# A list scheduler's cost table: the drain of an instruction booked as latency, and a short look ahead on each engine

## The chip, the cores and the metric

The kernel runs on one core of a Trainium2 chip. The metric is the device time of one launch in microseconds (us), the median of several runs. Engines are named as in the profile: PE is the matrix engine (PEld its weight loads), DVE the vector engine, ACT the scalar engine, POOL the GpSimd engine, SP the sync engine, which issues nearly all DMAs here.

## The reference

One layer of a hybrid decoder serves 256 prompt tokens and 8 sequences of 8 new tokens, 320 tokens in all, with D_MODEL 2048. One wide projection feeds two recurrent branches, each branch is projected back, and the two are merged by gates:

```python
h = rms_norm(x, norm_g)
p = jnp.einsum('nld,dp->nlp', h, w_in)          # 2048 -> 11392 columns
...
y_a, s_a_new = rwkv7_recurrence(r_h, heads_a(decay), k_h, v_h, kk, heads_a(a), s_a)
...
o_b, s_b_new = gla_chunkwise(heads_b(q_b, DK_B), heads_b(k_b, DK_B), heads_b(i_b, DV_B),
                             heads_b(log_g, DK_B), s_b)
...
merged = (jax.nn.sigmoid(p[..., OFF_GA:OFF_GB].astype(f32))
          * jnp.einsum('nlw,wd->nld', y_a.astype(dt), proj_a)
          + jax.nn.sigmoid(p[..., OFF_GB:].astype(f32))
          * jnp.einsum('nlw,wd->nld', y_b.astype(dt), proj_b))
y = x + jnp.einsum('nld,de->nle', merged.astype(dt), w_out)
```

## The kernel before

All big products are made with three passes of a reduced float type: a weight tile `raw` (1024 rows by 128 columns, 512 KB) is loaded by SP, ACT casts it to its high part `whi`, DVE subtracts to get the low part `wlo`, and PE multiplies high by high, high by low and low by high. One such half tile is a block of 24 matmuls into a PSUM tile `mps`. These 320-column matmuls are called stream matmuls here.

The program has four stages. In the start stage the input is normalized and transposed and a first tile is made. In the recorded stage eight rounds run, p = 0 to 7. Each projects eight column tiles (r, k, v, za, q, f, i, zb: sixteen blocks) and then has the work of both branches for that round: `rwkv(p, ...)` for two heads of branch A and `hgrn(p, ...)` for one head of branch B. That work is a long chain of small steps: small matmuls and transposes on PE into the PSUM tiles `a`, `b` and `y`, with DVE, ACT and POOL steps between them. Seven gate tiles follow. In the third stage the remaining gates, proj_a (`ppa`), proj_b (`ppb`) and the merge are made, from lines 362 to 364 (matmuls), 352 (cast) and 353 (subtraction). The last stage is the output projection (`po`) and the final norm.

Only the recorded stage is ordered by a planner, class `Recorder`. It records every call of a round on every engine (all carry line 1465, where the recorded calls are issued again) and then orders them once, before the program is built:

- `add` gives each operation a cost (how long it holds its engine) and a latency `lat` (how much later a reader on its result may start).
- `link` builds the dependences. An edge marked as data adds the latency. `rank` is the longest way to the end.
- `order` is a list scheduler. `choose(e)` picks for engine e the next operation: for PE a ready small matmul, otherwise the next stream matmul; for the other engines, among the operations that could start within 30 ns of the earliest one, the one with the greatest `worth`. Worth puts the weight split of a block first when fewer than 4500 ns of stream matmuls are left ahead of it, then the operation with the greatest rank, and splits that are not urgent last.
- `OVER` says how early an operation may start on the SBUF port that DVE and POOL share, `MARGIN` is 250 ns added in front of a small matmul.

What the planner emits is a fixed order for each engine. The engines run through their own orders on the chip and wait for one another by semaphores, so a planned time that is wrong changes nothing by itself; it only puts an instruction in a worse place. PE has its stream matmuls to fill the time that a chain of branch work needs: the number of stream matmuls that stand between two dependent small matmuls is the cover of the steps between them.

Names that the text below uses: `uE<-a`, `uB<-a`, `pp`, `yz`, `yd` belong to a triangular solve of branch A that goes back and forth between PE and the other engines; `dn`, `pp<-scr`, `y`, `ye` are a small inverse in the same branch whose pieces are rearranged by two round trips through DRAM (`scr<-dn` then `pp<-scr`, and `scr<-y` then `ye<-scr`), after which POOL writes `yd` and PE transposes it (`a<-ident,yd`).

Of the kernel before, what the change touches and what calls it, by code (L numbers as in the profile page):

```python
# [67 lines left out]


class Recorder:  # L70
    APART, MARGIN, WAIT, OVER = 10, 250, 6000, 130
    LAT = {"PE": 215, "V": 45, "S": 45, "G": 80, "Y": 0}

    def __init__(self, engines, is_big):
        self.real, self.ops, self.spans, self.is_big = engines, [], {}, is_big
# [10 lines left out]
    def add(self, eng, name, fn, args, kw):  # L86
        o = Op()
        o.eng, o.fn, o.args, o.kw, o.n = eng, fn, args, kw, len(self.ops)
        aps = [x for x in (*args, *kw.values()) if hasattr(x, "start_partition")]
        out = aps[0]  # L90
        free = 1
        for d in out.shape[1:]:
            free *= d
        o.uses = []
        for j, x in enumerate(aps):
            t_ = x.tensor
            if "DRam" in type(t_).__name__:
                if t_.name.startswith("scr"):
                    o.uses.append((t_.name, 0, 1, 1, j == 0, False))
                continue  # L100
            key = (t_.name, x.offset, tuple(map(tuple, x.ap)))
            if key not in self.spans:
                self.spans[key] = span_of(x)
            o.uses.append((*self.spans[key], j == 0, "PSUM" in str(x.space)))
        o.lat = self.LAT[eng]
        o.dma = "dma" in name
        o.mode = None
        o.block, o.group = self.block, self.group
        o.margin, o.wait = 0, self.wait

        two = sum("PSUM" not in str(x.space) for x in aps[1:] if tuple(x.shape[1:]) != (1,)) > 1
        o.hold = two and eng in "VG"
        o.port = two and eng == "V" or eng == "G" and "dma" not in name
        if eng == "PE":
            lhs, rhs = aps[1], aps[2]
            o.cols = 1
            for d in lhs.shape[1:]:
                o.cols *= d
            n = 1
            for d in rhs.shape[1:]:  # L120
                n *= d
            up = lambda x: 32 if x <= 32 else 64 if x <= 64 else 128
            o.mode = up(lhs.shape[0]), 128 if name == "transpose" else up(o.cols)
            one = name == "transpose" or lhs.dtype == F32R
            o.passes = 1 if one else 2
            load = o.cols / 1.2
            stream = n / 2.4 + 13 if one and lhs.dtype == F32R else 2 * n / 2.4
            side = 128 // o.mode[1] * (128 // o.mode[0] if o.group else 1)
            o.cost = o.passes * max(max(load, stream) / side, 7) if o.group else o.passes * max(load, stream / min(2, side))
            if o.mode == (128, 128) and n > 256:  # L130
                o.cost = o.passes * stream
            o.stream = self.is_big(out)
            o.margin = 0 if o.stream else self.MARGIN
        elif eng == "V":
            two = name in ("tensor_scalar", "tensor_copy") and all(not u[5] for u in o.uses)
            o.cost = (free / 2 if two else free) / 0.96 + (150 if two else 157)
            if two:
                o.hold = o.port = True
            if any(tuple(x.shape[1:]) == (1,) and free > 1 for x in aps[1:]):
                o.cost += 55  # L140
            if name == "tensor_tensor_scan":
                o.cost = 2 * free / 0.96 + 157
        elif eng == "S":
            o.cost = (150 if name == "copy" else 200) + free / 1.2
            if name == "copy" and not o.uses[1][5]:
                o.cost += 40
            if any(tuple(x.shape[1:]) == (1,) and free > 1 for x in aps[1:]):
                o.cost += 60
        elif eng == "G":
            o.cost = 950 if "dma" in name else 95 + free * 0.88 if name == "memset" else 200 + free * 1.66  # L150
            if "dma" in name:
                o.lat = 4500
        else:
            o.cost, o.lat = 380, 2600 if any(u[0].startswith("scr") for u in o.uses) else 5500
        self.ops.append(o)
        return o

    def link(self):
# [42 lines left out]
        for o in self.ops:  # L201
            o.npred = len(preds[o.n])
            for q, data in preds[o.n].values():
                q.succ.append((o, data))
        for o in reversed(self.ops):
            o.rank = o.cost + max((q.rank + (o.lat if data else 0) for q, data in o.succ), default=0)
        for members in groups.values():
# [4 lines left out]
    def order(self):  # L212

        self.link()
        free = dict.fromkeys(self.real, 0.0)
# [7 lines left out]
        port = {"V": 0.0, "G": 0.0}  # L223
# [6 lines left out]
        def choose(e):  # L230

            q = ready[e]
            now = free[e]
            if e in port:
                held = port["G" if e == "V" else "V"] - self.OVER
                if e == "V" and held > now and port["G"] == free["G"]:

                    held += min((o.cost for o in ready["G"] if o.hold and o.ready <= free["G"] - 40), default=0.0)
                at_ = {o: max(now, o.ready, held if o.port else 0.0) for o in q}
                t_ = min(at_.values())  # L240
            else:
                t_ = max(now, min(o.ready for o in q))
            if e == "PE":
                can = [o for o in q if o.ready <= t_ + 1]
                own = [o for o in can if o.mode == mode and not o.stream]
                part = [o for o in can if o.mode != (128, 128)]
                if mode != (128, 128):
                    near = [o for o in q if o.mode == mode and o.ready <= t_ + 60]
                    pool = own or near or part or can
                elif own:  # L250
                    pool = own
                elif part and (run_ >= self.APART and any(t_ - o.ready >= o.wait for o in part) or len(part) == len(can)):
                    pool = part
                else:
                    pool = [o for o in can if o.stream]
                o = max(pool, key=lambda o: (o.rank, -o.n))
                if o.stream:
                    o = min((o for o in pool if o.stream), key=lambda o: o.n)
                return max(t_, o.ready), o
            can = [o for o in q if (at_[o] if e in port else o.ready) <= t_ + 30]  # L260

            def worth(o):
                if o.block is None:
                    return (3 if e == "Y" else 1), o.rank
                slack = (at[o.block] - gone) * 147 + max(0, free["PE"] - t_)
                return (2 if slack < 4500 else 0), -o.n
            return t_, max(can, key=worth)

        while left:
            t_, o = min((choose(e) for e in ready if ready[e]), key=lambda x: (x[0], x[1].eng == "V"))  # L270
# [1413 lines left out]
```

## Time and profile before

| | us |
|---|---|
| runs: median (lowest to highest of 3) | 1105.28 (1103.35 to 1106.14) |
| the profiled execution | 1104.54 |
| its span, first to last instruction | 1102.8 |
| PE busy | 1081.3 |
| DVE busy | 750.6 |
| ACT busy | 680.1 |
| POOL busy | 154.6 |

The profiled execution took 1.7 us more than its span, which lies outside its first and last instruction. Busy times are unions over an engine's instructions, so two that overlap are counted once. The recorded stage lies at about 27 to 690 us, the third stage follows to about 1000 us, the output projection after that. In a row of the timeline the first number is the start, the second the length, and a bracket at the end gives the idle time ahead of the row and what ended it.

### The profile page before, as it was taken

What the parts mean: (1) busy time and instruction counts of PE and PEld (TensorE: products, weight loads), DVE (VectorE), ACT (ScalarE), POOL (GpSimd) and SP (SyncE); (2) the same over time, 40 slices, a digit from 0 to 9 for tenths busy, and PEclk for the clock granted to TensorE, in tenths of its full rate; (3) what the DMA queues carried; (4) which work ended last, traced back from release to release, by engine and by line L of the source; (5) the groups of instructions that cost most, each with busy time, mean ns of one, the idle gap of its engine ahead of it and who ended that gap; (6) DMA issues with size and microseconds to landing.
All of it is one profiled execution on the core that took longest, in us unless ns stands there. A gap on an engine that the chain in (4) does not pass through costs nothing.

```text
span 1102.8 us, 23134 instructions
## 1 busy us (share of the span) xinstructions
PE 1081.3 (98%) x9020; PEld 1043.5 (95%) x9020; DVE 750.6 (68%) x1639; ACT 680.1 (62%) x1530; POOL 154.6 (14%) x328
## 2 busy tenths in 40 slices
PE   7999999999999999999999999999999999999996
PEld 6999999999998999999999999999999999998886
DVE  8878787888787788788887976644444444437532
ACT  8767776766865867857857867544444444435412
POOL 6421222311211211211311210000000000000000
PEclk9999999999999999999999999999999999999999
DMA  6743644654553554555445454555555555586502
GB/s 200 205 127 100 180 129 123 161 145 114 162 136 101 156 144 117 153 138 140 117 138 144 123 144 130 149 152 160 152 146 146 149 154 153 153 282 223 200 21 96
DMA packets 298386, 161.62 MB, mean 147 GB/s; under 512 B 37341, under 2 KB 288480, under 8 KB 297700
## 3 DMA queue, kind: packets, MB, share of 16 engines
q1 hardware_dynamic: 297908, 158.83, 50.1%
q8 instruction: 71, 1.16, 0.4%
q10 hardware_dynamic: 368, 1.31, 0.3%
q14 instruction: 39, 0.32, 0.1%
HBM read 149.41 MB, written 10.70 MB: 145 GB/s over the span
## 4 chain that ended last, share of the span: by engine, by line
PE 95%; ACT 2%; DMA 1%; DVE 1%; issue 0%; POOL 0%; DVEq 0%; SPq 0%; ACTq 0%
PE mps L1465 45%; PE a L1465 9%; PE mps L362 5%; PE mps L364 5%; PE mps L363 5%; PE b L1465 3%; PE po L1555 3%; PE po L1556 3%; PE po L1557 3%; PE ppa L363 2%; PE ppa L364 2%; PE ppa L362 2%; PE ppb L362 2%; PE ppb L363 2%; PE ppb L364 2%; PE y L1465 1%
## 5 line engine op out<-in xcount | busy, mean ns | idle before, releaser
L1465 PE MATMUL mps<-hhi,wlo 128*128 128x320 f32 x1136 | 358.9, 316 | 0.0
L1465 PE MATMUL mps<-hhi,whi 128*128 128x320 f32 x1136 | 357.0, 314 | 0.5 <-ACT pad L1465 0.5
L1465 PE MATMUL mps<-hlo,whi 128*128 128x320 f32 x1136 | 357.3, 314 | 0.0
L1465 PEld LDWEIGHTS mps<-hhi,wlo 128*128 128x128 f32 x1136 | 213.7, 188 | 2.3 <-issue 1.5
L1465 PEld LDWEIGHTS mps<-hhi,whi 128*128 128x128 f32 x1136 | 213.8, 188 | 2.0 <-issue 0.8
L1465 PEld LDWEIGHTS mps<-hlo,whi 128*128 128x128 f32 x1136 | 213.7, 188 | 1.5 <-issue 0.8
L1465 DVE TENSOR_TENSOR wlo<-raw,whi 128x1024 fp32r<-128x1024 f32 x140 | 173.6, 1240 | 21.0 <-ACT whi L1465 19.7
L1465 ACT CAST whi<-raw 128x1024 fp32r<-128x1024 f32 x140 | 146.4, 1045 | 63.2 <-PE mps L1465 56.7
L352 ACT CAST whi<-raw 128x1024 fp32r<-128x1024 f32 x82 | 86.0, 1049 | 147.8 <-PE mps L363 94.3
L353 DVE TENSOR_TENSOR wlo<-raw,whi 128x1024 fp32r<-128x1024 f32 x82 | 100.5, 1225 | 110.1 <-ACT whi L352 110.1
L362 PE MATMUL mps<-hhi,whi 128*128 128x320 f32 x400 | 123.9, 310 | 1.0 <-ACT whi L352 1.0
L364 PE MATMUL mps<-hhi,wlo 128*128 128x320 f32 x400 | 123.7, 309 | 0.2 <-DVE wlo L353 0.2
L363 PE MATMUL mps<-hlo,whi 128*128 128x320 f32 x400 | 123.8, 309 | 0.0
L362 PEld LDWEIGHTS mps<-hhi,whi 128*128 128x128 f32 x400 | 75.1, 188 | 1.3 <-ACT whi L352 1.3
L364 PEld LDWEIGHTS mps<-hhi,wlo 128*128 128x128 f32 x400 | 75.1, 188 | 0.4 <-DVE wlo L353 0.4
L363 PEld LDWEIGHTS mps<-hlo,whi 128*128 128x128 f32 x400 | 75.2, 188 | 0.0
L1544 DVE TENSOR_TENSOR wlo<-raw,whi 128x1024 fp32r<-128x1024 f32 x32 | 38.4, 1222 | 36.0 <-ACT whi L1543 35.8
L1543 ACT CAST whi<-raw 128x1024 fp32r<-128x1024 f32 x32 | 33.1, 1052 | 47.7 <-PE po L1560 21.1
L1555 PE MATMUL po<-whi,mhi 128*128 128x512 f32 x128 | 50.0, 391 | 0.0
L1556 PE MATMUL po<-whi,mlo 128*128 128x512 f32 x128 | 50.0, 391 | 0.0
L1557 PE MATMUL po<-wlo,mhi 128*128 128x512 f32 x128 | 50.0, 391 | 0.0
L362 PE MATMUL ppa<-yah,whi 128*128 128x320 f32 x128 | 40.1, 314 | 0.1
(444 smaller groups left out, 2100.2 us busy)
## 6 DMA issues: line engine op xcount, KB each, us to landing
raw<-in_w_in_dram SPq DMA_DIRECT2D x194, 512.0 KB
raw<-in_w_out_dram SPq DMA_DIRECT2D x32, 512.0 KB
raw<-in_proj_a_dram SPq DMA_DIRECT2D x16, 512.0 KB
raw<-in_proj_b_dram SPq DMA_DIRECT2D x16, 512.0 KB
s<-in_state_hgrn_dram SPq DMA_DIRECT2D x8, 512.0 KB
out_dram<-s SPq DMA_DIRECT2D x8, 512.0 KB
s<-in_state_rwkv_dram SPq DMA_DIRECT2D x8, 256.0 KB
out_dram<-s SPq DMA_DIRECT2D x8, 256.0 KB
```

The costliest lines, as they stand in the source:

```text
L352: S.copy(hi[:, ks], raw[:, ks])
L353: sub.tensor_sub(lo[:, ks], raw[:, ks], hi[:, ks].bitcast(F32))
L362: T.matmul(dst, hi[:, q, :], xhi[:, k, :], start=(k == 0), stop=False)
L363: T.matmul(dst, hi[:, q, :], xlo[:, k, :], start=False, stop=False)
L364: T.matmul(dst, lo[:, q, :], xhi[:, k, :], start=False, stop=(k == nk - 1))
L1465: o.fn(*o.args, **o.kw)
L1543: S.copy(hi, raw)
L1544: V.tensor_sub(lo, raw, hi.bitcast(F32))
L1555: T.matmul(pt, h, hi, start=first, stop=False)
L1556: T.matmul(pt, l, hi, start=False, stop=False)
L1557: T.matmul(pt, h, lo, start=False, stop=end)
```

## The change

In the table of `Recorder`, the cost of a DVE, ACT or POOL instruction is lowered by 85, 100 or 65 ns (`DRAIN`), and the same number is added to its latency. The latencies themselves are trimmed from 45, 45 and 80 ns to 40, 40 and 65. `OVER` goes from 130 to 45, which is the same point in time, since the end that it is counted from is 85 ns earlier. `tensor_reduce` is now charged for the elements that it reads, not only for those that it writes.

In `link`, an edge from a DVE, ACT or POOL operation to another engine always carries the latency, also where only a buffer is handed back.

In `choose`, an engine other than PE now looks 150 ns ahead (`AHEAD`, before 30). When the operation with the greatest worth is ready only later than 30 ns from now, one that is ready and will be done at most 60 ns (`SLIP`) after that point goes first; if there is none, the engine is kept free for it. No operation is added or removed.

```diff
-    APART, MARGIN, WAIT, OVER = 10, 250, 6000, 130
-    LAT = {"PE": 215, "V": 45, "S": 45, "G": 80, "Y": 0}
+    APART, MARGIN, WAIT, OVER = 10, 250, 6000, 45
+    AHEAD, SLIP = 150, 60
+    LAT = {"PE": 215, "V": 40, "S": 40, "G": 65, "Y": 0}
+    DRAIN = {"V": 85, "S": 100, "G": 65}
...
+        if eng in self.DRAIN and not o.dma:
+            if name == "tensor_reduce":
+                n = 1
+                for d in aps[1].shape[1:]:
+                    n *= d
+                o.cost += (n - free) / 0.96
+            o.cost -= self.DRAIN[eng]
+            o.lat += self.DRAIN[eng]
...
-                q.succ.append((o, data))
+                q.succ.append((o, data or q.eng in self.DRAIN and q.eng != o.eng))
...
-            can = [o for o in q if (at_[o] if e in port else o.ready) <= t_ + 30]
+            if e not in port:
+                at_ = {o: max(now, o.ready) for o in q}
...
-            return t_, max(can, key=worth)
+            best = max((o for o in q if at_[o] <= t_ + self.AHEAD), key=worth)
+            if at_[best] > t_ + 30:
+                short = [o for o in q if at_[o] <= t_ + 30 and at_[o] + o.cost <= at_[best] + self.SLIP]
+                if short:
+                    best = max(short, key=worth)
+            return t_, best
```

The recorded calls keep their number, and their lines move by 16 (1465 becomes 1481, 352 becomes 368). Three places show what the planner makes of it.

On PE, in round 7 of 8, the triangular solve alternates between `a<-pp,uB` and `a<-yz,uE`. Before, the rows there read:

```order
L1465 MATMUL a_496<-yz,uE_504 128x128 x2
L1465 MATMUL mps<-hhi,wlo 128x320
L1465 MATMUL a_497<-pp_515,uB_501 128x128 x2
L1465 MATMUL mps<-hhi,whi 128x320
L1465 MATMUL mps<-hlo,whi 128x320
L1465 MATMUL a_496<-yz,uE_504 128x128 x2
L1465 MATMUL a_498<-ident,yd 128x128 x2
```

The same two steps from `a<-pp,uB` to `a<-yz,uE` on PE in the changed program:

```order
L1481 MATMUL a_497<-pp_515,uB_501 128x128 x2
L1481 MATMUL mps<-hlo,whi 128x320
L1481 MATMUL mps<-hhi,wlo 128x320
L1481 MATMUL mps<-hhi,whi 128x320
L1481 MATMUL mps<-hlo,whi 128x320
L1481 MATMUL b_526<-ident,i_487 128x128 x3
L1481 MATMUL mps<-hhi,wlo 128x320
L1481 MATMUL mps<-hhi,whi 128x320
L1481 MATMUL a_496<-yz,uE_504 128x128 x2
L1481 MATMUL a_498<-ident,yd 128x128 x2
```

Between the two steps stood two stream matmuls; now there stand six and three transposes of branch B. Ahead of `a<-pp,uB` stood one stream matmul, now eleven. At the same step of round 6, where two stream matmuls stood between `a<-pp,uB` and `a<-yz,uE` a second time, now stand fourteen. The new order repeats itself: in rounds 2 to 7 these distances are the same each time, which they were not before.

On DVE, in round 3, the small inverse is nine steps from `y<-id,pp` to the second reduction. Before, from the first of them:

```order
L1465 TENSOR_TENSOR y_0_517<-id_146,pp_515 96x64
L1465 TENSOR_TENSOR F_529<-F_529 128x16x8
L1465 TENSOR_TENSOR pp_515<-y_0_517 96x4
L1465 TENSOR_TENSOR w_0_524<-w_0_524,f_485 128x320
L1465 TENSOR_TENSOR wlo<-raw,whi 128x1024
L1465 TENSOR_TENSOR y_0_517<-y_0_517,pp_515 96x2x2
L1465 TENSOR_TENSOR R_530<-R_530,F_529 128x8x16
L1465 TENSOR_TENSOR pp_515<-y_0_517 96x4
```

DVE in the changed program, round 3, the whole inverse and a row on either side:

```order
L1481 TENSOR_TENSOR wlo<-raw,whi 128x1024 x2
L1481 TENSOR_TENSOR y_0_517<-id_146,pp_515 96x64
L1481 TENSOR_TENSOR pp_515<-y_0_517 96x4
L1481 TENSOR_TENSOR y_0_517<-y_0_517,pp_515 96x2x2
L1481 TENSOR_TENSOR pp_515<-y_0_517 96x4
L1481 TENSOR_TENSOR y_0_517<-y_0_517,pp_515 96x2x2
L1481 TENSOR_TENSOR pp_515<-y_0_517 96x64
L1481 TENSOR_REDUCE p_0_518<-pp_515 96x16
L1481 TENSOR_TENSOR pp_515<-y_0_517,p_0_518 96x64
L1481 TENSOR_REDUCE y_0_517<-pp_515 96x4x4
L1481 TENSOR_TENSOR q_483<-q_483,w_0_524 128x320
```

Two weight splits (`wlo`) and eight other steps stood among the nine; now they stand ahead of them and behind them. The stretch of PE that this chain has to fit into, from the `a<-arp,bk` that it starts from to the first `a<-ident,yd`, held 130 stream matmuls in round 1 and 159 to 174 in rounds 2 to 8; now it holds 127 in rounds 1 to 7 and 120 in round 8. On SP a `raw` load stood between `scr<-y` and `ye<-scr` in six of the eight rounds and between `scr<-dn` and `pp<-scr` in three; now it does in eight and in seven.

On ACT, at the end of the recorded stage, the last steps of round 8 (the group norm, `uB`) stood among the first casts of the third stage (line 352):

```order
L1465 ACTIVATE f_485<-mps 128x320
L1465 COPY uE_504<-a_496 128x320
L1465 ACTIVATE f_485<-f_485 128x320
L1465 ACTIVATE uB_501<-a_496 128x320
L1465 ACTIVATE f_485<-f_485 128x320
L1465 CAST rh_494<-uB_501 128x320
L1465 COPY ks_537<-b_527 100x128
L352 CAST whi<-raw 128x1024
L1465 ACTIVATE uB_501<-a_497,eps_g 128x320
L1465 ACTIVATE uB_501<-uB_501 128x320
L352 CAST whi<-raw 128x1024
L1487 CAST yah<-ya 128x640 x4
```

ACT in the changed program, up to the same split of `ya` (line 1503 now):

```order
L1481 CAST whi<-raw 128x1024 x2
L1481 ACTIVATE za_481<-mps 128x320
L1481 ACTIVATE za_481<-za_481 128x320 x2
L1481 CAST whi<-raw 128x1024
L368 CAST whi<-raw 128x1024
L1481 ACTIVATE q_483<-mps 128x320
L1481 ACTIVATE q_483<-q_483 128x320 x2
L368 CAST whi<-raw 128x1024 x2
L1481 ACTIVATE f_485<-mps 128x320
L1481 ACTIVATE f_485<-f_485 128x320 x2
L368 CAST whi<-raw 128x1024
L1503 CAST yah<-ya 128x640 x4
```

The last branch work has left this place: on PE the last small matmul stood behind 76 stream matmuls of the third stage, and now stands 226 stream matmuls ahead of the end of the recorded ones. The number of times that PE changes between its full and its divided array is 64 in both programs.

## The prediction

> **What bounds the kernel now.** I read the page first, then the table of windows, then PE's own timeline at each place where a window shows it idle.
>
> ```profile
> PE 1081.3 (98%) x9020; PEld 1043.5 (95%) x9020; DVE 750.6 (68%) x1639; ACT 680.1 (62%) x1530; POOL 154.6 (14%) x328
> PE 95%; ACT 2%; DMA 1%; DVE 1%; issue 0%; POOL 0%; DVEq 0%; SPq 0%; ACTq 0%
> 125.00:300.00 175.00, 173.96 (x1673) 170.28 (x1672) 144.79 (x360) 128.72 (x324) 38.71 (x76) 1.00 0.49 137
> 300.00:400.00 100.00, 98.12 (x926) 96.13 (x925) 80.15 (x197) 72.99 (x187) 24.16 (x46) 1.00 0.47 130
> 400.00:600.00 200.00, 197.92 (x2059) 192.61 (x2058) 163.30 (x438) 140.68 (x366) 38.15 (x78) 1.00 0.50 138
> 600.00:700.00 100.00, 98.09 (x894) 94.98 (x893) 74.96 (x174) 78.03 (x188) 11.74 (x22) 0.98 0.49 138
> 680.00:700.00 20.00, 18.60 (x196) 17.17 (x195) 12.62 (x21) 13.80 (x27) 0.00 (x0) 0.91 0.48 139
> ```
>
> PE is busy for 98% of the span and is 95% of the chain that ended last, so the kernel is bound by the matrix engine and the change removes no matmul. The order can win only PE's idle time. In a window row the columns are length, then busy time of PE, PEld, DVE, ACT and POOL, then PE's granted clock. From 125 to 700 us PE is idle for 1.04 + 1.88 + 2.08 + 1.91 = 6.9 us, and the granted clock falls below 1 in one place, 0.91 in 680 to 700. DVE is busy 144.79 of 175 us, 83%: not a bound, but close enough that the order of its queue decides when a result is there. The idle time lies in nine stops:
>
> ```profile
> 248.52 0.44 PE L1465 MATMUL a<-ident,yd 128*128 128x128 f32 x2 [1.04 <-POOL yd L1465]
> 248.72 0.39 PE L1465 MATMUL mps<-hhi,whi 128*128 128x320 f32 x1
> ...
> 345.12 0.25 PE L1465 MATMUL b<-ks,s 128*32 128x64 f32 x2 [1.88 <-issue]
> ...
> 497.25 0.71 PE L1465 MATMUL a<-yz,uE 128*128 128x128 f32 x4 [0.57 <-DVE yz L1465]
> 498.42 0.41 PE L1465 MATMUL mps<-hhi,whi 128*128 128x320 f32 x1 [0.46 <-ACT pad L1465]
> ...
> 572.16 0.68 PE L1465 MATMUL a<-pp,uB 128*128 128x128 f32 x4 [0.41 <-issue]
> 573.86 0.71 PE L1465 MATMUL a<-yz,uE 128*128 128x128 f32 x4 [0.64 <-DVE yz L1465]
> ...
> 673.59 0.49 PE L1465 MATMUL a<-uv,bk 128*128 128x128 f32 x2 [0.50 <-ACT uv L1465]
> ...
> 689.72 0.31 PE L364 MATMUL mps<-hhi,wlo 128*128 128x320 f32 x1
> 691.92 0.31 PE L364 MATMUL mps<-hhi,wlo 128*128 128x320 f32 x1
> 693.22 0.41 PE L362 MATMUL mps<-hhi,whi 128*128 128x320 f32 x1 [0.99 <-ACT whi L352]
> 694.48 0.41 PE L364 MATMUL mps<-hhi,wlo 128*128 128x320 f32 x1 [0.22 <-DVE wlo L353]
> 695.70 0.47 PE L363 MATMUL ppa<-yal,whi 128*128 128x320 f32 x1
> 698.10 0.47 PE L363 MATMUL ppa<-yal,whi 128*128 128x320 f32 x1
> ```
>
> Between 689.72 and 691.92 lie 15 steps of stream matmuls, 0.147 us each, while a row shows a length of 0.31. So a stop costs its listed idle time and the overlap that it loses, 0.31 - 0.147 = 0.16 us. Between 695.70 and 698.10 nine steps take 0.267 us each: that is the stretch of lower clock.
>
> **The change part by part.** *Drain as latency.* The rows that decide whether this is true of the chip:
>
> ```profile
> 233.14 0.22 DVE L1465 TENSOR_TENSOR y<-id,pp 96x64 f32<-96x64 f32 x1
> ...
> 233.49 0.15 DVE L1465 TENSOR_TENSOR pp<-y 96x4 f32<-96x4 f32 x1
> 233.56 0.48 DVE L1465 TENSOR_TENSOR w<-w,f 128x320 f32<-128x320 f32 x1
> 233.96 1.22 DVE L1465 TENSOR_TENSOR wlo<-raw,whi 128x1024 fp32r<-128x1024 f32 x1
> 235.09 0.15 DVE L1465 TENSOR_TENSOR y<-y,pp 96x4 f32<-96x4 f32 x1
> ...
> 690.53 0.49 DVE L1465 TENSOR_TENSOR uE<-uE,uB 128x320 f32<-128x320 f32 x1
> 691.06 0.45 DVE L1465 TENSOR_SCALAR uE<-uE,cols 128x320 f32<-128x320 f32 x1
> ```
>
> The instruction at 233.56 lasts 0.48 us, and the next, which does not need it, starts 0.40 later; the 1.22 us one is followed after 1.13. Where the second needs the first (690.53), it starts 0.53 after a 0.49 us one. So 0.08 to 0.09 us of a DVE instruction's end are latency and not occupancy, as the new table has it. The old one planned DVE as if each of its instructions held it that much longer, took weights and operands for later than they are, and placed small matmuls close behind their producers where it thought no stream matmul was ready. A dependent chain by itself costs nearly the same in both tables (490 + 45 ns before, 405 + 125 now for 320 columns). The trimmed latencies, the dearer `tensor_reduce` and the latency on handed-back buffers act through the order alone, so their price is in the stops below.
>
> The Trainium skill, "VectorE: DVE Perf Modes", section "The DRAIN you can't avoid", speaks against the change: the next op does not start until the pipeline has emptied. By that rule the old cost was the right one. The rows above contradict it here, and the page itself sends the reader to its section on two instructions with no wait between them, where an op that is not held starts earlier.
>
> *The four stops at 497 to 574.* They cost 0.57 + 0.46 + 0.41 + 0.64 = 2.08 and 4 x 0.16, 2.72 us. From `a<-pp,uB` at 572.16 to `a<-yz,uE` at 573.86 are 1.70 us. The new order has the pair itself (0.44 as at 248.52), six stream matmuls (0.88) and three transposes (0.3, by the two that take 0.20 from 248.52 to 248.72): 1.62 in place of 0.90, so 0.08 of this stop is left. At 497.25 twelve more stream matmuls are 1.76 us against 0.73; at 572.16 ten more are 1.47 against 0.57. The one at 498.42 waits for a PSUM tile that ACT empties; I take it as gone with its neighbours, and as kept for the range (0.62).
>
> *The stop at 673.59*, 0.66 us, is the end of round 8, which now runs under 226 recorded stream matmuls: gone.
>
> *The junction to the third stage.* 0.99 + 0.22 + 2 x 0.16 = 1.53 us, waits for a cast and a split that ACT and DVE did between the last steps of round 8. Those steps have left. What is late next is the split of `ya` itself, four casts that stand ahead of a weight cast in both orders, so up to the whole 1.53 may stay.
>
> *The stretch of lower clock.* From 695.4 to 698.6, 12 matmuls lose 0.12 us each, 1.4; by the window (0.09 of 20 us) it is 1.8. I take 1.6 as gone with the stops ahead of it. A stop of 1.88 us at 345.12 brought none, so this is not certain: 0 to 1.6.
>
> The Trainium skill, "TensorE: Matmul & The Clock Gate", Part 1, has the half clock follow an idle window of about 3.4 us that runs freely. The length fits, but no such idle time precedes it here. By that rule these stops were not its cause, and the sum would be 1.6 us smaller.
>
> *The inverse and its round trips.* This is where the change spends cover.
>
> ```profile
> 62.39 0.27 PE L1465 MATMUL a<-arp,bk 64*128 64x128 f32 x1
> 72.16 0.21 DVE L1465 TENSOR_TENSOR y<-id,pp 96x64 f32<-96x64 f32 x1
> 75.82 0.56 SPq L1465 DMA_DIRECT2D scr<-y  x1
> 81.57 0.66 POOL L1465 TENSOR_TENSOR yd<-ye,seqm 128x256 f32<-128x256 f32 x1 [14.26 <-DMA ye<-scr]
> 82.86 0.38 PE L1465 MATMUL a<-ident,yd 128*128 128x128 f32 x2
> ...
> 160.11 0.33 SPq L1465 DMA_DIRECT2D scr<-y  x1
> 165.41 0.92 POOL L1465 TENSOR_TENSOR yd<-ye,seqm 128x256 f32<-128x256 f32 x1 [14.72 <-DMA ye<-scr]
> ...
> 239.35 0.33 SPq L1465 DMA_DIRECT2D scr<-y  x1
> 241.67 0.37 SPq L1465 DMA_DIRECT2D raw<-in_w_in_dram  x1
> 242.36 0.37 SPq L1465 DMA_DIRECT2D ye<-scr  x1
> 247.22 1.25 POOL L1465 TENSOR_TENSOR yd<-ye,seqm 128x256 f32<-128x256 f32 x1 [2.35 <-DMA ye<-scr]
> ```
>
> The first five rows are round 1. From `a<-arp,bk` at 62.39 to `a<-ident,yd` at 82.86 PE had 20.47 us under 130 stream matmuls; POOL was done at 82.23, so the chain needed 19.9. With 127 the stretch is 3 x 0.147 shorter, 20.0 us; I reckon with 19.8, since a few of the small matmuls in it have moved as well. In the other rounds it held 159 to 174, 23.4 to 25.6 us of stream matmuls alone, so the change takes 4 to 6 us of cover from each. What pays for it are the nine DVE steps in one piece. In round 3 the split at 233.96 alone held the next of them from 233.64 to 235.09, and from 233.14 to `scr<-y` at 239.35 the nine took 6.2 us; in round 1 they took 72.16 to 75.82, 3.7. Nine steps of 0.15 to 0.28 with 0.03 between them are 2.0. So the chain of round 1 would need 19.9 - 1.7 = 18.2 us. It fits, as long as the second round trip is a short one: from `scr<-y` to POOL 5.75 us in round 1 and 5.3 in round 2, but 7.9 in round 3, where a 512 KB load stood between and POOL's step took 1.25 instead of 0.66. With the long trip it needs 18.2 + 2.1 = 20.3, 0.5 over the cover, and with POOL's longer step 1.1. The new order has that load in between in every round. I count three long trips of the eight, two at 0.5 and one at 1.1: 2.1 us given back, an estimate from these rows; and the stop at 248.52 (1.04 + 0.16 = 1.20), which is this chain, as gone. The range holds none and eight.
>
> *Keeping an engine free* costs at most 0.15 us of DVE or ACT each time, in an engine with 17% to spare; nothing by itself. The trace has no row of it: between nothing and the round-trip price above. The stop at 345.12 (2.04) has no releaser in the trace and stays. The other stages are not planned and stay.
>
> **Sum.** 2.72 - 0.08 + 0.66 + 1.53 + 1.6 + 1.20 = 7.6 us gone, 2.1 given back: 5.5 off 1104.54, which is 1099.0. The profiled execution lies 0.7 under the median of the runs and within their spread, so I leave it there.
>
> **Rivals.** (1) *All stops go and nothing comes back.* 1104.5 - 7.6 = 1096.9. The regular order speaks for it, the tight cover against. (2) *The thinner covers give most of it back.* A wait of 0.7 us at the inverse in each of eight rounds, 5.6: 1102.5, no change that can be told, since a measurement of this kernel tells about 0.3%, 3.3 us, from none. (3) *Slower by the round trips.* Since all rounds now have one pattern, a collision is paid in all. The first trip, `scr<-dn` to `pp<-scr`, has a weight load in between in seven rounds as well, three before. If both trips land like the long one in each round, the chain needs 18.2 + 2 x 2.1 + 0.6 = 23.0 us for 19.8, 3.2 x 8 = 25.6: 1104.5 - 7.6 + 25.6 = 1122.5. It decides from (7.6 + 3.3) / 8 = 1.4 us a round. Against it: with loads in between in six rounds PE stopped for `yd` once. (4) *The drain is occupancy after all.* Then each queued DVE instruction is 0.085 late; with ten of them in front of a result, at two tight places a round, 16 x 0.85 = 13.6 against the 7.6: 1110.5. The rows at 233.56 and 233.96 nearly exclude it. This is what the rule of the VectorE page would bring. (5) That the change does nothing is out: the orders differ from the first round on.
>
> **How the numbers follow.** Forecast 0.57 (own range 1097 to 1101.9), (1) 0.12, (2) 0.20, (3) 0.08, (4) 0.03. Faster by over 0.3% are the forecast and (1), 0.69; within it (2), 0.20; slower (3) and (4), 0.11. The range reaches from below (1) into the upper part of (2), 1095.5 to 1105.5; outside are (3), (4) and some 0.07 at the two edges.
>
> **What would show it.** PE without idle time at the solve's `a<-yz,uE`; the granted clock 1.00 through the junction; no wait for `whi` at the first casts of the third stage; DVE's nine steps in about 2 us; the last small matmul some 33 us ahead of the last recorded stream matmul. If PE waits for POOL `yd` in most rounds, (2) or (3) is true. I am wrong at the root if PE's busy time itself moves, or if new waits for `wlo` or `whi` stand inside the recorded stage.

## The result, and the profile after

The changed kernel takes 1134.91 us (median of 4 runs, 1132.96 to 1136.44); the kernel before 1105.07 (4 runs, 1103.35 to 1106.14). The ratio is 1.0271 with a 95% interval of [1.025, 1.0291]: 2.7% slower, where 1099.0 us was forecast. Nothing in the range from 1095.5 to 1105.5 is near it.

Two lines of the page of after, busy time and the shares of the chain that ended last:

```profile
PE 1100.5 (97%) x9020; PEld 1043.8 (92%) x9020; DVE 753.5 (67%) x1639; ACT 691.4 (61%) x1530; POOL 144.3 (13%) x328
PE 65%; DVE 14%; ACT 12%; DMA 3%; issue 3%; POOL 1%; SPq 0%; DVEq 0%; ACTq 0%; POOLq 0%
```

PE does the same 9020 matmuls and is busy 19.2 us longer (1081.3 before), and the chain now runs through DVE and ACT for a quarter of the span (2% + 1% before). The first had been named as the sign of an error at the root. The windows of after, the last of them around the junction to the third stage, which now comes at 724 us, some 30 us later than before:

```profile
125.00:300.00 175.00, 170.24 (x1621) 161.36 (x1619) 143.37 (x369) 126.17 (x314) 36.23 (x83) 1.00 0.46 129
300.00:400.00 100.00, 97.61 (x891) 92.76 (x888) 77.65 (x191) 71.17 (x172) 17.74 (x36) 1.00 0.49 134
400.00:600.00 200.00, 194.46 (x1990) 182.62 (x1989) 161.20 (x422) 149.06 (x388) 35.15 (x76) 1.00 0.46 126
720.00:740.00 20.00, 19.17 (x129) 18.68 (x128) 13.77 (x18) 12.81 (x20) 0.00 (x0) 1.00 0.58 169
```

Read the counts, not the busy time. From 125 to 300 us PE issued 1621 matmuls where it had issued 1673, 3.1% fewer, and from 300 to 600 us 2881 for 2985. (A short window can mislead, since a count rises where many short matmuls fall in it; over these 475 us it does not matter much.) Its idle time in the first row rose by 3.7 us, from 1.04 to 4.76, which is only 2.1% of the window. A matmul's end in this trace is modelled, so part of a short wait is drawn as a longer neighbour. That is how PE's busy time moved while its work stayed the same: it is wait, not work. PE's waits in the trace of after, with the total, the number and the longest:

```profile
PE a L1481 <- DVE uv L1481: 6.4, 8, 0.9
...
PE a L1481 <- DVE v L1481: 2.4, 6, 0.5
PE a L1481 <- DVE g L1481: 2.3, 7, 0.5
PE a L1481 <- POOL yd L1481: 1.2, 4, 0.6
PE b L1481 <- DVE o L1481: 1.1, 7, 0.2
...
PE ppa L379 <- DVE yal L1504: 0.4, 1, 0.4
...
PE ppa L378 <- ACT yah L1503: 0.4, 1, 0.4
```

Short waits, six to eight of most kinds, so about one a round, at places where the kernel before stood once or never. By an estimate a round now loses some 5 us: against the summed work of PE's own instructions the first stream matmul came 4.0 us late in round 2, 19.2 in round 5 and 39.5 at the gate tiles (before: 0.1, 1.7 and 7.0). The estimate takes the work of each kind of matmul from stretches of the trace of before in which PE does not wait.

### Where one of these waits comes from

ACT's timeline in after, ahead of one of the longest waits for `uv`:

```profile
414.76 0.40 ACT L1481 ACTIVATE s<-s,dec 128x128 f32<-128x128 f32 x1
415.06 0.23 ACT L1481 COPY att<-attc 32x64 f32<-32x64 f32 x1
415.30 1.07 ACT L1481 CAST k<-b 32x128 fp32r<-32x128 f32 x4
416.39 0.40 ACT L1481 ACTIVATE s<-s,dec 128x128 f32<-128x128 f32 x1
416.82 0.22 ACT L1481 ACTIVATE uv<-a 64x64 f32<-64x64 f32 x1
```

DVE and PE beside it:

```profile
416.40 0.29 DVE L1481 TENSOR_TENSOR k<-b,k 32x128 fp32r<-32x128 f32 x1 [0.47 <-ACT k L1481]
417.07 0.22 DVE L1481 TENSOR_SCALAR uv<-a 64x64 f32<-64x64 f32 x1 [0.20 <-ACT uv L1481]
...
416.18 0.31 PE L1481 MATMUL mps<-hhi,wlo 128*128 128x320 f32 x1
417.35 0.49 PE L1481 MATMUL a<-uv,bk 128*128 128x128 f32 x2 [0.86 <-DVE uv L1481]
```

The first `s` lasts 0.40 us, and `att` starts 0.30 after it: an overlap of 0.10, as the new table has it. The four casts do not overlap. They take 1.07 us, 0.27 each, and `s` starts 0.02 after the last of them has ended. The new table gives such a cast 150 + 128/1.2 - 100 = 157 ns. So the four casts are 0.44 us behind the plan, `s` (planned 267 ns) 0.16 more; DVE waits 0.47 for `k`, then 0.20 for `uv`, and PE, which has no more than the stream matmuls that the plan thought enough, stands for 0.86 us. What marks the casts: they read PSUM tile `b` at partition 64, 96, 64 and 96, while `att` and the first `s` start at partition 0. The second `s` writes at partition 0 behind a cast that wrote at 64.

The trace of before shows the same two kinds side by side on ACT:

```profile
425.71 0.19 ACT L1465 COPY rhs<-y 64x64 f32<-64x64 f32 x1
425.81 0.40 ACT L1465 ACTIVATE s<-s,dec 128x128 f32<-128x128 f32 x1
426.24 0.37 ACT L1465 COPY ket<-b 128x256 f32<-128x256 f32 x1
426.50 0.33 ACT L1465 COPY uK<-y 128x192 f32<-128x192 f32 x1
...
429.54 0.80 ACT L1465 CAST k<-b 32x128 fp32r<-32x128 f32 x3
430.36 0.40 ACT L1465 ACTIVATE s<-s,dec 128x128 f32<-128x128 f32 x1
```

`rhs` reads PSUM from partition 64; `s` touches no PSUM and starts 0.09 before its end. `ket` is the next to read PSUM, now from partition 0, and starts 0.03 after the end of `s`; `uK`, again from 0, overlaps. The three casts take 0.27 each here as well. So it was in the trace before the change was made.

Counted over the recorded stage, in pairs of neighbours on an engine where the second does not need the first and had its other operands at least 0.25 us earlier, the two kinds split by one condition: an instruction is **held** until the one before has ended if its input starts in another group of 32 partitions than the last input read from that memory (SBUF or PSUM), or its output in another group than the last output written there. The counts are of the pairs that behave as the condition says, the times the median distance from the end of the one to the start of the next, from the trace's starts and lengths:

```
              not held          held             split as the condition says
before DVE    585   -83 ns      319   +31 ns     904 of 913
before ACT    515   -98 ns      313   +24 ns     828 of 831
after  DVE    537               330              867 of 883
after  ACT    384               316              700 of 700
```

The Trainium skill, "VectorE: DVE Perf Modes", section "Two Vector instructions with no wait between them", states this condition for VectorE; the trace agrees in 904 of 913 pairs. The 85 and 100 ns are thus true of two instructions in three; for the others the new table is about 114 ns (DVE, 83 + 31) or 122 ns (ACT, 98 + 24) too cheap.

The distances of the held ones fall into two groups that do not overlap, and what divides them is whether the instruction ahead signals a semaphore when it ends. A narrower count over the recorded stage of before takes only the pairs where the trace shows when each wait ended. All of them, 721 on DVE and 627 on ACT, split by the condition:

```
                                  DVE                        ACT
not held                          441   -82 ns               365   -98 ns
held, the one ahead signals none  127   +14 (13 to 15)       122   +12 (11 to 12)
held, the one ahead signals       153   +31 (30 to 32)       140   +25 (23 to 26)
```

So a held instruction costs some 17 ns (DVE) or 13 ns (ACT) more behind one that signals, and the +31 and +24 above are medians of a mixture.

### The profile page after: what moved, and what is told of

Its sections match the earlier page's. It is cut to its first block, busy times and chain, and to the rows that moved or that the text cites. A ratio compares the mean times of both kernels' runs of the same rounds, so it can differ in the third digit from the quotient of the medians.

```text
span 1131.9 us, 23151 instructions
## 1 busy us (share of the span) xinstructions
PE 1100.5 (97%) x9020; PEld 1043.8 (92%) x9020; DVE 753.5 (67%) x1639; ACT 691.4 (61%) x1530; POOL 144.3 (13%) x328
## 3 DMA queue, kind: packets, MB, share of 16 engines
q8 instruction: 70, 1.15, 0.4%
## 4 chain that ended last, share of the span: by engine, by line
PE 65%; DVE 14%; ACT 12%; DMA 3%; issue 3%; POOL 1%; SPq 0%; DVEq 0%; ACTq 0%; POOLq 0%
PE mps L1481 23%; PE mps L378 5%; PE mps L379 5%; PE mps L380 5%; DVE wlo L1481 4%; PE a L1481 4%; PE po L1571 3%; PE po L1572 3%; PE po L1573 3%; DMA ye<-scr 2%; ACT whi L1481 2%; PE ppa L379 2%; PE ppb L378 2%; PE ppb L379 2%; PE ppb L380 2%
## 5 line engine op out<-in xcount | busy, mean ns | idle before, releaser
L379 PE MATMUL ppa<-yal,whi 128*128 128x320 f32 x128 | 39.7, 310 | 0.4 <-DVE yal L1504 0.4
```

What stands on the lines that cost most here:

```text
L379: T.matmul(dst, hi[:, q, :], xlo[:, k, :], start=False, stop=False)
```

## The experiments

Each kernel was timed in turn with the kernel before, on the same chip; ratios are to that one.

### Which half of the change

e1 has only the new costs and latencies (in after.py `AHEAD = 30`, which is the old choice). e2 has only the look ahead.

```diff
 e1:
-    AHEAD, SLIP = 150, 60
+    AHEAD, SLIP = 30, 60
 e2:
-    APART, MARGIN, WAIT, OVER = 10, 250, 6000, 45
+    APART, MARGIN, WAIT, OVER = 10, 250, 6000, 130
-    LAT = {"PE": 215, "V": 40, "S": 40, "G": 65, "Y": 0}
-    DRAIN = {"V": 85, "S": 100, "G": 65}
+    LAT = {"PE": 215, "V": 45, "S": 45, "G": 80, "Y": 0}
+    DRAIN = {}
```

> Costs as in the change, looking ahead set back from 150 to 30 ns. Theory A (the drain is credited also to instructions that the chip holds until the one before has ended, so DVE and ACT are planned too fast and PE is given too little cover): as slow as the change, 1122 to 1142 us, with PE's waits spread over many small matmuls in every round. Theory B (keeping an engine free for the longest step idles it): the loss goes, at most 1110 us. Theory C (the round trips through DRAM are what comes too late): as slow as the change, but with most of the waiting at the transposes of yd.

> Costs, latencies and OVER as before, looking ahead 150 ns as in the change (the charge for tensor_reduce and the latency on handed-back buffers are left out with them). Theory A: no credit is taken, so there is no loss; 1094 to 1108 us, and some of the nine stops of before may go. Theory B: slower than before by 10 us or more, 1115 us and up. Theory C: about 1105 us, nothing in it touches the round trips.

e1: 1145.43 us, ratio 1.0346 [1.0323, 1.0369]. e2: 1097.46 us, 0.9922 [0.99, 0.9945]. With the kernel before at 1 and the change at 1.0271 this is a square whose sides agree: the costs lose 3.5% without the look ahead and 3.5% with it, the look ahead gains 0.8% with either table. So theory B, that an engine kept free loses the time, is out. Windows of e2:

```profile
125.00:300.00 175.00, 174.89 (x1692) 171.18 (x1691) 149.31 (x368) 134.44 (x333) 37.24 (x83) 1.00 0.50 138
300.00:400.00 100.00, 100.00 (x931) 98.38 (x930) 84.07 (x209) 74.35 (x186) 18.23 (x39) 1.00 0.52 142
400.00:600.00 200.00, 199.83 (x2076) 195.37 (x2075) 168.81 (x430) 148.00 (x376) 41.16 (x84) 1.00 0.49 132
```

PE has 0.28 us of idle time in 475, and in each row it issues more matmuls than in the kernel before and in the change. In e1 PE's waits are these, with POOL's `yd` first:

```profile
PE a L1481 <- POOL yd L1481: 7.2, 8, 1.7
...
PE a L1481 <- DVE yz L1481: 3.9, 11, 0.4
PE a L1481 <- DVE rl L1481: 3.5, 7, 0.5
PE a L1481 <- ACT uv L1481: 3.0, 7, 0.4
```

### Does the held instruction do it

e3 is the change with a planner that knows held instructions: `add` keeps for each operation the groups of 32 partitions in which its operands start, and `order` starts one that changes group later by 110 ns (DVE) or 122 ns (ACT). e4 leaves the costs alone and only adds 350 ns in front of each small matmul.

```diff
 e3:
+    HELD = {"V": 110, "S": 122}
...
+            if o.eng in last:
+                r, w = last[o.eng]
+                if any(r.get(m, k) != k for m, k in o.reads) or any(w.get(m, k) != k for m, k in o.write):
+                    return free[o.eng] + self.HELD[o.eng]
+            return free[o.eng]
 e4:
-    APART, MARGIN, WAIT, OVER = 10, 250, 6000, 45
+    APART, MARGIN, WAIT, OVER = 10, 600, 6000, 45
```

> The change, and the planner now knows when the credit doesn't hold: an instruction on DVE or ACT that reads or writes from another group of 32 partitions than the last one that read or wrote the same memory starts 110 (DVE) or 122 ns (ACT) after the cost of the one before, so it gets the drain back and 22 to 25 ns. Theory A: the loss goes, and with it most stops: 1093 to 1106 us, PE's excess over its own work in the recorded stage under 12 us (40 in the change, 12.5 before). Theory B and C: within 8 us of the change, 1127 us and up.

> The change with MARGIN at 600 in place of 250 ns: every small matmul is placed 350 ns of PE work further behind its operands, nothing else. Theory A: cover is what is missing, some 0.1 us for each held instruction in a chain, so most of the loss comes back: 1100 to 1118 us. Theory B: the engines stay idle as often, the time stays at 1127 us or more. Theory C: the trips are late by more than 350 ns, so less than a third of the loss comes back, 1125 us and up.

e3: 1103.85 us, 0.9972 [0.9959, 0.9986]: of the 3.5% between the change and e2, 3.0 come back (33 us), with the drain still booked as latency wherever instructions overlap. Theories B and C gave it 1127 us and more. The dearer `tensor_reduce`, the trimmed latencies and the latency on handed-back buffers are all in e3 too, so together they are worth no more than the 0.5% that is left. PE's waits for `uv`, `v`, `g` and `o` fall from 12.2 us to 0.2; the largest left in the recorded stage are:

```profile
PE a L1500 <- POOL yd L1500: 1.9, 1, 1.9
...
PE b L1500 <- issue: 1.0, 1, 1.0
```

e4: 1125.08 us, 1.0166 [1.0149, 1.0183], above what theory A gave it and at the number of theory C (the round trips through DRAM). C falls by e3, which leaves the round trips as they are. The 0.35 us in front of each small matmul buy less than a third of the loss. A reading that no run tests: a margin covers one late step, while every held instruction of a chain adds its 0.1 us and pushes all that is queued behind it. PE now waits elsewhere:

```profile
PE b L1481 <- DVE o L1481: 4.3, 5, 0.9
...
PE a L1481 <- POOL yd L1481: 3.1, 3, 1.4
```

### One engine at a time, half the credit, and the instruction by itself

```diff
 the change:
-    DRAIN = {"V": 85, "S": 100, "G": 65}
 e5:
+    DRAIN = {"V": 85}
 e6 (with OVER = 130):
+    DRAIN = {"S": 100}
 e7 (with OVER = 87):
+    DRAIN = {"V": 42, "S": 50, "G": 32}
 e8, in the output stage, on DVE (tensor_add) and on ACT (copy):
+            for way in ("none", "read", "write", "both", "chain"):
+                for j in range(4):
+                    r = Q[j % 2] if way in ("read", "both") else Q[0]
+                    w = Q[j % 2] if way in ("write", "both") else Q[0]
+                    put(probe[w, c:c + 12], probe[r, c - 12:c] if way == "chain" else src[r])
```

> Only DVE's cost is lowered by 85 ns; ACT's and POOL's costs are the old ones. Theory A (an instruction that changes the 32-partition group of its input or output has to wait for the end of the one before it, on DVE and on ACT alike, and is planned about 110 or 122 ns too early): with these two numbers on the held instructions of this very order, PE loses 17 us against e2_ahead_only, so about 1115 us (1112 to 1121, since the same working gave 34 of the 37 us of the change and 23 of the 28 of e4). Theory D (whatever plans tighter loses in proportion to what is credited, held or not): DVE's and ACT's shares together are the 37 us, about 1116 each. Theory E (only DVE holds, ACT's drain is latency as booked): the whole loss, 1135.

> Only ACT's cost is lowered by 100 ns. Theory A: by the same working PE loses 12 us against e2_ahead_only, about 1110 us (1107 to 1115). Theory D: about 1116. Theory E: nothing, 1097.5 us (1095 to 1100).

> Every credit halved: 42, 50 and 32 ns, with the port number moved to match. The mean over held and unheld instructions is then about right, and only the pattern is missing. Theory A: what is late on a held instruction is partly made up by the unheld ones around it; by the same working PE loses 6 us against e2_ahead_only, about 1103.5 us (1101 to 1108). Theory D: half the loss, 18.7 us, about 1116.

> The changed kernel with 20 short instructions (32 x 12) on DVE and 20 on ACT in the output stage, four each way, none of the first sixteen needing another: input and output in one group of 32 partitions; input alternating between two groups; output alternating; both alternating; and last four of which each reads the one before. The time of the whole is of no interest. Theory A: on both engines an instruction of the first four starts some 80 to 100 ns before the one ahead of it has ended, and those of the three alternating sets 20 to 30 ns after it has ended, so about 110 ns further apart on DVE and 122 ns on ACT. Theory E: DVE so, on ACT all sixteen overlap. If grouping by partitions is only a companion of something else in the kernel, all sixteen are alike.

e8 shows the mechanism by itself, in one execution. The profile has each set of 20 as one row, with the shortest, median and longest length:

```profile
L1629 DVE TENSOR_TENSOR probe<-probe x20: 151/159/166, 1104.6 to 1107.6; 32x12 f32<-32x12 f32 x20
L1636 ACT COPY probe<-probe x20: 194/199/203, 1104.7 to 1108.3; 32x12 f32<-32x12 f32 x20
```

The twenty are nearly equally long, 151 to 166 ns on DVE and 194 to 203 on ACT; what differs is the distance. From the starts in the trace, medians of the three pairs inside each set:

```
ns                    DVE start to start, end to start     ACT start to start, end to start
one group             84       -70                          103       -93
input alternates      171      +14                          211       +12
output alternates     171      +14                          212       +12
both alternate        174      +14                          211       +11
each needs the last   194      +35                          232       +32
```

A change of group costs 87 ns on DVE and 108 on ACT, whether the input or the output changes, and with both at once (90 and 108) no more to speak of. That is less than the 110 and 122 that e3 books from the kernel: in the first four sets no instruction ahead of another signals, so these are the short distances of the table above. Theory E, that only DVE does this, is out; e6 says the same, where ACT's credit alone loses.

e5: 1115.09 us, 1.008 [1.0065, 1.0095]. e6: 1118.96, 1.0116 [1.0099, 1.0133]. e7: 1110.75, 1.0045 [1.003, 1.006]. These three do not tell A and D (loss in proportion to the credit, held or not) apart: e5 fits both, e6 and e7 are slower than A gave them (e6 is nearer to D, e7 lies midway), and the losses of e5 and e6 add up to that of the change as D has it. D falls by e3 against e7. By the shares counted above, e3 credits 46 ns (DVE) and 54 ns (ACT) on the mean, 85 and 100 on the two thirds and minus 25 and 22 on the rest; e7 credits 42 and 50 on every instruction. For nearly the same sum e3 loses 5.5 us against e2 and e7 13.6: it matters which instructions get the credit. The estimate behind A is the planner's own table with the 110 and 122 ns, applied to each kernel's order as it stands; without them the same working finds no loss in any of these orders:

```
lost against e2 (us)       e1     change   e4     e5     e6     e7
by the held instructions   30.8   34.4     22.8   17.3   12.2   6.0
measured                   46.9   38.6     27.0   17.5   21.5   13.6
```

(Measured: the ratio less 0.9922, times 1106 us.) It accounts for nine tenths of the change's loss, but for less than half of that of e7; in e1, e6 and e7 8 to 16 us remain which it does not have.

### POOL, the look ahead, and the last 0.5%

e3 is still 0.5% above e2. Suspected first was POOL: in after, e2 and e3 its steps keep the next one waiting some 0.2 us longer than the change's table has it. e9, e10, e11 and e12 plan them longer; e10 is e9 without the look ahead.

```diff
 e9 (e3), e10 (e3 with AHEAD = 30), e12 (the change):
-            o.cost = ... else 200 + free * 1.66
+            o.cost = ... else 400 + free * 1.66
 e11 (e2):
+            o.cost = ... else 340 + free * 1.66
```

> e3_held with each POOL step planned 200 ns longer: in the traces of after, e2 and e3 a POOL step keeps the next one waiting 199 to 231 ns longer than the table has it. Theory F (what e3 still loses against e2_ahead_only, 6.4 us, is POOL's wrong cost; the steps of this very order, re-timed with POOL's 200 ns, lose 6.8 us in e3 and 0.1 here): 1097.5 us (1095 to 1100.5), PE's waits for `yd` gone. Theory R (e3 loses because a table that is exact leaves no reserve for what varies from round to round): 1102 to 1106, as e3.

> e9_held_pool with AHEAD back at 30 ns, so the engines are no longer kept free for the step with the longest way to the end. If keeping free is what gains (theory K, from e2_ahead_only): branch work falls behind again, the last small matmul stands behind all recorded stream matmuls as before the change, and the time is 1102 us or more (to 1115). If true costs alone give the gain: as e9_held_pool within 2 us.

> e2_ahead_only (the old costs and latencies, with the look ahead) with each POOL step planned 140 ns longer, which is the same POOL time as in e9_held_pool. PE's loss in e2 is 2.7 us, of which some 0.6 by the re-timing are POOL's: theory F expects 1096.9 us (1095 to 1098.5), theory R nothing to be told from e2_ahead_only.

> The change with each POOL step planned 200 ns longer and nothing else. Theory A (instructions that change the group of partitions): those are still planned too early, re-timed PE loses 24 to 29 us against e2_ahead_only, so 1121.5 to 1127 us. If POOL's cost and not the held instructions is the cause of the loss: 1098 to 1104.

e9: 1103.43 us, 0.9969 [0.9955, 0.9983]; e11: 1099.39, 0.9932 [0.9918, 0.9946]; e12: 1131.07, 1.0219 [1.02, 1.0238]. PE's waits for `yd` do go in e9, and the time does not: theory F is out for e3. In the change POOL's cost is worth half a per cent, and e12 is still above what A gave it; to e2 it is worth nothing. e10: 1121.87, 1.0128 [1.0104, 1.0152], above the range given. With true costs the look ahead is worth 1.6%: without it the branch work falls behind and ends at the third stage again, as in the kernel before. PE waits there; the window of 680 to 700 us has 254 matmuls where a stretch of stream matmuls alone has 138, so small ones are still among them:

```profile
PE ppa L397 <- ACT yah L1522: 4.0, 1, 4.0
...
680.00:700.00 20.00, 18.42 (x254) 16.17 (x254) 14.11 (x44) 14.58 (x47) 2.14 (x2) 1.00 0.44 127
700.00:720.00 20.00, 14.57 (x166) 12.61 (x166) 13.66 (x24) 13.61 (x31) 0.00 (x0) 0.91 0.28 77
```

What was left is the reserve. e13 is e3 with 40 ns less credit on every DVE and ACT instruction; e14 is e2 again, on the same chip.

```diff
 e13 (e3):
-    DRAIN = {"V": 85, "S": 100, "G": 65}
+    DRAIN = {"V": 45, "S": 60, "G": 65}
```

> e3_held with 40 ns less credit on every DVE and ACT instruction (45 and 60 in place of 85 and 100), the held ones known as before: each is planned 40 ns longer than it is. Theory R (an exact table leaves no reserve, so each step that is late is paid by PE): the 6 us that e3 loses against e2_ahead_only come back, 1096 to 1100 us. If something else than the missing reserve holds e3 back (theory S: its order, the places where its small matmuls stand): 1102 to 1106 as before.

> The kernel of e2_ahead_only once more, on the same chip as e13_held_reserve: 1096 to 1099 us, 0.990 to 0.994 of the kernel before. If the first result was of that chip alone: nearer to 1.

e13: 1098.5 us, 0.9927 [0.9914, 0.994]; e14: 1096.95, 0.9916 [0.9903, 0.9929]. This is what theory R gave, and not S: with 40 ns in hand on each instruction the table with held instructions comes to about 0.1% of e2. From 400 to 600 us its PE is as full; from 125 to 400 it has 1.5 us of idle time, e2 0.1. It is one order, so a lucky one is not excluded:

```profile
400.00:600.00 200.00, 200.00 (x2088) 195.36 (x2087) 169.78 (x436) 153.02 (x392) 40.75 (x91) 1.00 0.51 138
```

A reading of why the old table does well: it had both in one. Its 85 and 100 ns too much on two instructions in three paid for the 31 and 24 ns too little on the third, with some left over. The fastest version is therefore the smallest edit, the look ahead with the old table: 0.8% under the kernel before, in two series on two chips.

## Why the prediction was wrong

**The bound** was read rightly, nearly: the order can win only PE's waits, but not all of them are idle time. In e2 PE's idle time is 5.0 us less than before and its busy time 2.3 us less, for the same matmuls. 7.6 us were to be had by the sum; the look ahead alone gained 0.8%, 9 us, and e2 at 1097 lies between the forecast and its first rival. The stops that the prediction struck out inside the recorded stage are gone in e2, and so is the one at 345.12, which it kept (one of 0.6 us, for `rl`, is new). The gain that was forecast is real and belongs to the other half of the change.

**Drain as latency** is the step that failed: "So 0.08 to 0.09 us of a DVE instruction's end are latency and not occupancy, as the new table has it." Two rows carried it, 233.56 and 233.96. Both instructions, and those that follow them, start at partition 0: they are of the two thirds that overlap. The trace held 319 DVE pairs of the other kind and 313 on ACT, of which the prediction shows no row at all. A rule for every instruction of three engines was taken from two instructions of one. In its place the runs show that one instruction in three starts only 12 to 31 ns after the end of the one ahead of it. Planned as the others these come 0.11 to 0.12 us too early, and that is most of the 38.6 us between e2 and the change: with them known to the planner, 33 us come back (e3).

**The weighing of the Trainium skill** went wrong in the same place. The section that has an op wait for the pipeline was set aside by those rows, and the one it points to was named without asking which ops are held. Rival 4 (1110.5, chance 0.03) was right in direction; it was priced with DVE alone and two tight places a round, where the lateness arises on two engines and is paid at six or more places. The rows that "nearly exclude it" exclude it for themselves.

**The stops.** The four at 497 to 574 are gone as such: PE's list of waits in after has none for `yz` or `pad`, and `uB` is down to 0.5 us in three stops of the whole program. The one at 673.59 was taken as gone with the rest of round 8, and most of it is still there, 0.4 us at the same step (`uv`). PE's waits of after from 640 to 700 us:

```profile
PE b L1481 <- ACT s L1481: 0.7, 1, 0.7
PE a L1481 <- DVE uv L1481: 0.4, 1, 0.4
```

The end of round 8 has more stream matmuls behind it now, and the matmul is still placed too soon after its producer.

**Junction and clock** came out as the prediction allowed, not as its sum has it. The waits for a cast and a split have left, and the split of `ya` is what is late next, at 724 us: 0.39 + 0.44 us, with the overlap that each loses 1.15 of the 1.53 that the sum counts as gone. 720 to 740 us shows the full clock. The stretch of lower clock has gone with the longer stops, as chosen, but the other runs do not bear out the stops as its cause. Where it appears, in before, e1, e3 and e10, it is 3.41 us at a granted clock of 0.50. e3 shows it behind stops of 1.1 + 0.4 us, e1 behind 1.4 + 0.4; e2 does not behind 0.7 + 0.4, but neither does e11 behind 1.6 + 0.5, longer than in e1 and e3. The window of e3:

```profile
680.00:700.00 20.00, 18.46 (x114) 17.97 (x113) 10.26 (x11) 12.24 (x20) 0.00 (x0) 0.91 0.55 158
```

**The inverse and its round trips.** The nine DVE steps in round 4 of after, first and last:

```profile
311.54 0.22 DVE L1481 TENSOR_TENSOR y<-id,pp 96x64 f32<-96x64 f32 x1 [1.41 <-DMA pp<-scr]
...
313.42 0.22 DVE L1481 TENSOR_REDUCE y<-pp 96x16 f32<-96x64 f32 x1
```

2.1 us, where about 2 were forecast, and PE's waits for `yd` come to 1.2 us in four stops, 1.8 with the overlap that each loses, against 2.1 forecast. This step and the rivals built on it (2 and 3) were not where the time went. In e1, without the look ahead, they would have been: `yd` costs 7.2 us there.

**Signs.** "I am wrong at the root if PE's busy time itself moves" was the one that spoke, 1081.3 to 1100.5 us.

Left open: the 8 to 16 us of e1, e6 and e7 that held instructions do not explain, and why stops of 1.1 and 1.4 us at the junction came with the lower clock (e3, e1) and one of 1.6 us did not (e11).

## What to carry to other kernels

Before a cost is moved from occupancy to latency, sort the trace's neighbouring pairs into those that overlap and those that do not, on each engine, and find what divides them; two rows that fit are no sample for a table that is applied to every instruction of three engines. In this kernel exact costs did a little worse than costs with a reserve: 40 ns on each instruction were worth 0.4% (e13 against e3), and a margin at the end of the chain did not replace right costs (e4). Where the busy time of the bound engine changes and its work does not, count its instructions over a long window: the waits are hidden in the lengths.

## What the hardware showed that was not expected

- ACT holds an instruction that changes the group of 32 partitions just as DVE does: 211 in place of 103 ns from start to start in e8, against 171 and 84 on DVE; an input or an output that changes has the same price, and both together no more.
- In e8 a held instruction starts 11 to 14 ns after the end of the one before, one that needs its result 32 to 35 ns after it. In the kernel (trace of before) a held one starts 13 to 15 (DVE) or 11 to 12 ns (ACT) after the end when the one ahead signals no semaphore, and 30 to 32 or 23 to 26 ns after it when it does: being held then costs nearly as much as a dependence.
- Instructions that do not change the group overlap by 70 ns (DVE) and 93 ns (ACT) even when they are only some 152 and 195 ns long (the first set of e8).
